# Half-size products for the first multiplication of two feed-forward steps of a one-core trunk

## The chip, the cores and the metric

One core of a Trainium2 chip runs the whole program in one launch. The metric is device time in microseconds, the median of several executions. "Before" is the kernel as it stands ahead of the change.

## The reference

The program is a two-layer trunk over 768 tokens (256 context tokens, then 512 latent tokens) with 1,024 channels. Each layer is a feed-forward half-step, a token mixer and a second feed-forward half-step. Layer 0 mixes by a diagonal state-space model (S5), layer 1 by gated linear attention (GLA). Around each of them stand an RMS norm and a modulation (scale, shift, gate) that comes from a product of a conditioning vector with `ada_w`. There are therefore four feed-forward steps. What matters here is

```python
def swiglu_ffn(h, w_in, w_out):
    gu = jnp.einsum('bld,df->blf', h, w_in)
    g, u = jnp.split(gu, 2, axis=-1)
    return jnp.einsum('blf,fd->bld', jax.nn.silu(g) * u, w_out)

def ffn_half_step(x, w_norm, shift, scale, gate, w_in, w_out):
    h = rmsnorm(x, w_norm) * (1.0 + scale) + shift
    return x + 0.5 * gate * swiglu_ffn(h, w_in, w_out)
```

with `w_in` 1,024 x 5,632 and `w_out` 2,816 x 1,024, all in 32-bit floats. Each operand of a large product is split into a rounded part and a remainder ("hi" and "lo"), and three matmuls (hi·hi, hi·lo, lo·hi) stand for one product.

## The kernel before

The activations lie transposed in SBUF: `xT` holds 8 tiles of 128 channels by 768 tokens. `Core.ffn` (L221) does one feed-forward step. It walks over 22 units of 128 hidden channels. `unit(j)` (L247) fetches the two weight tiles of a unit (gate and up, 128 x 1,024 each) by `weight` (L77): a DMA on the SP queue into one of four buffers `wraw`, a cast on ScalarE (L88) to a slot `whi`, and a subtraction on VectorE (L89) to a slot `wlo`. There are five slots of each kind, and three more while `core.more` is set, which it is from the S5 mixer's last product to the end of step three. `hidden(j, ...)` (L251) makes the gate and the up product of a unit for a stretch of tokens in two of the six PSUM banks, 8 x 3 matmuls each (`mm3`, L109 to L115), and then runs SiLU (L263), the product (L264), the cast (L265) and the remainder (L266). `products` (L268) multiplies the hidden channels of a group of units by `w_out` and adds the result to `xT` (L279). The units are taken in groups of four, twice in groups of two or four where the list `bounds` (L235) says so.

The first units, `lead` of them (4 with `core.more`), are made for thirds of the tokens (256 columns), so that they can begin on the first third while the norm of the others still runs. All later units work on halves (384 columns). The last group's second product is done third by third, and after each third the norm of the next step is queued.

That norm (`norm`, L186) squares the 8 tiles on ScalarE (L150) and adds the squares on VectorE (L151), forms the sums by a matmul with ones (L163), finds the inverse root in twelve small VectorE instructions (L167 to L175), spreads it over the partitions by a matmul (L182), scales (VectorE, L201), adds the shift and rounds (ScalarE, L218) and keeps the remainder (VectorE, L219). `later` and `tick` (L118 to L131) set where in the program these parts stand: so many ticks behind the third's last product. `ensure` forces them out before a unit reads their tokens.

Between the units a list of fillers runs (`fill`). In steps two and three they are the conditioning products, a block of 1,024 x 512 of `ada_w` each, done by `by_vector` (L416): four DMAs into `wraw` and 32 VectorE operations on it. Elsewhere the same blocks are done on TensorE (`block`, L410) by `ten(n)` (L1501). The S5 mixer ends in a recurrence on VectorE (`scan`, L824) and in `outputs` (L860), and then a gated product (`glu`, L921), whose last three of eight column groups are done third by third.

The framework orders the instructions of each engine ahead of time with a model of the timeline. The order in the program sets priorities, and the queues run in order on the chip.

## Time and profile before

| | us |
|---|---|
| median of 3 runs | 2894.43 |
| lowest, highest | 2892.82, 2896.95 |
| the profiled execution's own time | 2893.03 |
| its span | 2891.3 |

The profile is one execution. The time of an engine is "busy" only while an instruction runs on its data path. Matmuls overlap one another, so their rate is read from the distance of their starts and not from their duration. A line's idle time is the time its engine stood still just before it, put down to what came last. The work ahead of 998 us is step one, the S5 mixer and its gated product. Step two runs from 998 to 1554 us and step three from there to about 2125 us. GLA and step four follow.

### The profile page before, as it was taken

The page shows a single profiled execution, that of the slowest core. Times are in us where ns is not written, and L with a number is a line of the kernel's source. Part 1 is how long each engine was busy: PE and PEld are TensorE (multiplying, and loading weights), DVE is VectorE, ACT ScalarE, POOL GpSimd, SP SyncE. Part 2 cuts the span into 40 slices and gives each one's busy share as a digit, 9 for nine tenths or more (in the row PEclk, how much of TensorE's full clock was granted, in tenths as well). Part 3 has the DMA queues.
Part 4 walks back from the last instruction along what each step waited for, and adds up shares of the span by engine and source line. Part 5 has one row for each costly group of instructions (what it writes and reads, how often), then busy time and mean ns, then how long its engine had stood idle before and what let it go on. Part 6 is the DMA issues. An engine that isn't in the chain of part 4 may idle for free. (4 is left out here: it accounts for less than half of the span.)

```text
span 2891.3 us, 44942 instructions
## 1 busy us (share of the span) xinstructions
PE 2732.8 (95%) x18231; PEld 2581.4 (89%) x18231; DVE 1795.4 (62%) x4080; ACT 857.4 (30%) x1386; POOL 22.3 (1%) x57
## 2 busy tenths in 40 slices
PE   6999999996569999999999999999999999799998
PEld 5899999995459999999999999999988798788887
DVE  6699999536894565557527565665268786643433
ACT  4222222224363421111224221121246453332223
POOL 0000000000020000000000000000000000000000
PEclk9999999997789999999999999999999899799999
DMA  6545555526653133334211333333103112233330
GB/s 225 160 118 148 154 152 147 171 66 199 219 156 93 59 98 100 95 110 124 88 59 45 110 110 102 102 103 96 52 23 88 45 48 70 66 116 91 94 94 30
DMA packets 396044, 305.43 MB, mean 106 GB/s; under 512 B 57994, under 2 KB 344188, under 8 KB 395836
## 3 DMA queue, kind: packets, MB, share of 16 engines
q1 hardware_dynamic: 391228, 293.12, 34.7%
q10 hardware_dynamic: 4608, 9.44, 0.8%
q8 instruction: 143, 2.34, 0.3%
q14 instruction: 65, 0.53, 0.1%
HBM read 275.77 MB, written 30.41 MB: 106 GB/s over the span
## 5 line engine op out<-in xcount | busy, mean ns | idle before, releaser
L113 PE MATMUL bank<-h,whi 128*128 128x384 f32 (+3 forms) x3160 | 1044.7, 334 | 8.7 <-ACT whi L88 6.1
L114 PE MATMUL bank<-h,whi 128*128 128x384 f32 (+3 forms) x3160 | 1048.9, 333 | 0.0
L115 PE MATMUL bank<-h,wlo 128*128 128x384 f32 (+3 forms) x3160 | 1047.6, 332 | 0.0
L113 PEld LDWEIGHTS bank<-h,whi 128*128 128x128 f32 (+1 forms) x3160 | 593.9, 189 | 30.7 <-ACT whi L88 6.7
L88 ACT CAST whi<-wraw 128x1024 fp32r<-128x1024 f32 x313 | 327.4, 1048 | 966.3 <-PE bank L114 905.1
L114 PEld LDWEIGHTS bank<-h,whi 128*128 128x128 f32 (+1 forms) x3160 | 596.3, 189 | 17.2 <-issue 0.4
L115 PEld LDWEIGHTS bank<-h,wlo 128*128 128x128 f32 (+1 forms) x3160 | 595.1, 188 | 17.7 <-issue 0.7
L89 DVE TENSOR_TENSOR wlo<-wraw,whi 128x1024 fp32r<-128x1024 f32 x313 | 380.8, 1219 | 254.7 <-ACT whi L88 250.9
L114 PE MATMUL bank<-ml,whi 128*128 128x384 f32 (+2 forms) x1360 | 448.0, 330 | 0.0
L113 PE MATMUL bank<-mh,whi 128*128 128x384 f32 (+2 forms) x1360 | 445.7, 331 | 1.8 <-DVE xT L279 1.8
L115 PE MATMUL bank<-mh,wlo 128*128 128x384 f32 (+2 forms) x1360 | 446.2, 329 | 0.0
L279 DVE SCALAR_TENSOR_TENSOR xT<-bank,hg,xT 128x256 f32<-128x256 f32 (+2 forms) x488 | 221.4, 499 | 199.3 <-PE bank L115 198.8
L264 DVE TENSOR_TENSOR sg<-sg,bank 128x384 f32<-128x384 f32 (+2 forms) x166 | 89.4, 539 | 354.6 <-PE bank L115 339.2
L113 PEld LDWEIGHTS bank<-mh,whi 128*128 128x128 f32 x1360 | 256.3, 189 | 9.6 <-issue 2.8
L114 PEld LDWEIGHTS bank<-ml,whi 128*128 128x128 f32 x1360 | 256.9, 189 | 6.5 <-issue 0.4
L115 PEld LDWEIGHTS bank<-mh,wlo 128*128 128x128 f32 x1360 | 256.8, 189 | 6.2 <-issue 0.2
L427 DVE SCALAR_TENSOR_TENSOR adaacc<-wraw,cs,adaacc 128x512 f32<-128x512 f32 x336 | 236.9, 744 | 19.0 <-DMA wraw<-in_ada_w_dram 18.5
L265 ACT CAST mh<-sg 128x384 fp32r<-128x384 f32 (+2 forms) x166 | 83.5, 503 | 322.0 <-DVE sg L264 318.1
L263 ACT ACTIVATE sg<-bank 128x384 f32<-128x384 f32 (+2 forms) x166 | 79.5, 479 | 197.3 <-PE bank L115 195.1
L266 DVE TENSOR_TENSOR ml<-sg,mh 128x384 fp32r<-128x384 f32 (+2 forms) x166 | 89.8, 541 | 28.1 <-ACT mh L265 28.1
L150 ACT ACTIVATE sq<-xT 128x256 f32<-128x256 f32 (+1 forms) x126 | 52.0, 427 | 59.2 <-DVE xT L279 39.5
L201 DVE SCALAR_TENSOR_TENSOR nt<-xT,sc,bank 128x256 f32<-128x256 f32 (+2 forms) x136 | 61.8, 476 | 12.6 <-PE bank L182 9.7
(298 smaller groups left out, 2337.6 us busy)
## 6 DMA issues: line engine op xcount, KB each, us to landing
wraw<-in_ffn_w_in_dram SPq DMA_DIRECT2D x176, 512.0 KB, 4.2
wraw<-in_ada_w_dram SPq DMA_DIRECT2D x111, 512.0 KB, 4.0
wraw<-in_ffn_w_out_dram SPq DMA_DIRECT2D x88, 512.0 KB, 3.5
wraw<-in_gla_w_in_dram SPq DMA_DIRECT2D x24, 512.0 KB, 3.9
s5R<-s5r ACTq DMA_DIRECT2D x16, 512.0 KB, 4.9
s5O<-s5g SPq DMA_DIRECT2D x64, 128.0 KB, 3.8
wraw<-in_s_w_glu_dram SPq DMA_DIRECT2D x16, 512.0 KB, 6.5
big<-in_ada_w_dram SPq DMA_DIRECT2D x12, 512.0 KB, 8.8
```

What stands on the lines that cost most here:

```text
L88: nc.scalar.copy(out=hi[:, :n], in_=raw[:, :n])
L89: nc.vector.tensor_tensor(out=lo[:, :n], in0=raw[:, :n], in1=hi[:, :n].bitcast(F32), op=ALU.subtract)
L113: mm(out, wh, a[0], start=first, stop=False)
L114: mm(out, wh, a[1], start=False, stop=False)
L115: mm(out, wl, a[0], start=False, stop=last)
L201: nc.vector.scalar_tensor_tensor(out=t[:, a - s:z - s], in0=self.xT[:, k, a:z], scalar=sc[i][:, k:k + 1], in1=r[:, a - s:z - s], op0=ALU.m ...
L263: nc.scalar.activation(sg, banks[0][:, :e - s], AF.Silu)
L264: nc.vector.tensor_mul(sg, sg, banks[1][:, :e - s])
L265: nc.scalar.copy(out=mh[:, o], in_=sg)
L266: nc.vector.tensor_tensor(out=ml[:, o], in0=sg, in1=mh[:, o].bitcast(F32), op=ALU.subtract)
L279: nc.vector.scalar_tensor_tensor(out=self.xT[:, d, a:z], in0=banks[d][:, a - s:z - s], scalar=gate[i][:, d:d + 1], in1=self.xT[:, d, a:z], ...
L427: nc.vector.scalar_tensor_tensor(out=acc[:, v], in0=w[:, k], scalar=col, in1=acc[:, v], op0=ALU.mult, op1=ALU.add)
```

## The change

Steps two and three compute the first product by Strassen's scheme in Winograd's form: the weights of a unit are seen as a 2 x 2 block matrix (gate or up, by channels 0 to 511 or 512 to 1,023), the activations as a 2 x 2 block matrix (channel halves by even or odd blocks of 128 tokens). Seven half-size products (4 x 3 matmuls each) take the place of eight. A unit is done for all 768 tokens at once, 384 columns per matmul in three runs of 128, with each of the seven results in a bank of its own. GpSimd forms four sums of weight halves per unit, and in the norms ahead of the two steps it adds the squares and forms four differences of activations per half of a third. The sums of activations get a new buffer `hx`, and for it `core.more` goes: five weight slots of each kind stay. `lead` is 1, and the first unit is made for tokens 0 to 511 and then for 512 to 767. Blocks of `ada_w` are cut into four fillers each; steps two and three have six blocks each where they had eight, and the four others go to TensorE beside the S5 recurrence. The gated product's last part has two column groups where it had three.

```diff
+    def half(self, raw):
+        nc = self.nc
+        if self.pending is None:
+            self.pending = w = self.slot(True), self.slot(False)
+            hi, lo = (t[:, :HALF] for t in w)
+        else:
+            hi, lo = (t[:, HALF:] for t in self.pending)
+            self.pending = None
+        nc.scalar.copy(out=hi, in_=raw)
+        nc.vector.tensor_tensor(out=lo, in0=raw, in1=hi.bitcast(F32), op=ALU.subtract)
+        return hi, lo
...
-            nc.vector.tensor_add(acc, acc, sq)
+            (adds or nc.vector).tensor_tensor(out=acc, in0=acc, in1=sq, op=ALU.add)
...
+    def norm_seven(self, s, e, sc, sh, steps=0, gap=3):
+        acc = self.squares(s, e, nc.gpsimd)
...
+            for g in range(2):
+                v, w = (self.raw().rearrange("p (a i t) -> p a i t", i=2, t=t) for t in (2 * P, P))
+                for i in range(2):
+                    for lower in range(2):
+                        k, t = 4 * lower + 2 * g + i, v[:, lower, i]
+                        nc.vector.scalar_tensor_tensor(out=t, in0=self.xT[:, k, s:e], scalar=sc[:, k:k + 1], in1=r,
+                                                       op0=ALU.mult, op1=ALU.mult)
+                        nc.scalar.activation(t, t, AF.Identity, bias=sh[:, k:k + 1])
...
+                for x, minuend, less, (hi, lo) in ((b11, None, None, place(0, 0)), (t1, b12, b11, place(0, 1)),
+                                                   (t2, b22, t1, beside(0)), (b21, None, None, place(1, 0)),
+                                                   (t3, b22, b12, beside(1)), (b22, None, None, place(1, 1)),
+                                                   (t4, b21, t2, beside(2))):
+                    if less is not None:
+                        nc.gpsimd.tensor_tensor(out=x, in0=minuend, in1=less, op=ALU.subtract)
+                    nc.scalar.copy(out=hi, in_=x)
+                    nc.vector.tensor_tensor(out=lo, in0=x, in1=hi.bitcast(F32), op=ALU.subtract)
...
-        lead = 4 if self.more else 2
-        bounds = [0, 4, 8, 12, 14, 18, FT] if self.more else [0, 2, 6, 10, 14, 18, FT]
+        lead = 1 if seven else 4 if self.more else 2
+        bounds = [0, 4, 8, 12, 14, 18, FT] if self.more or seven else [0, 2, 6, 10, 14, 18, FT]
...
+            def both(out, i0, i1, op):
+                nc.gpsimd.tensor_tensor(out=out, in0=i0, in1=i1, op=op)
+                return self.half(out)
+            return [self.half(a11), both(a21, a21, a22, ALU.add), both(a11, a21, a11, ALU.subtract), self.half(a12),
+                    both(a21, a22, a11, ALU.subtract), both(a12, a12, a11, ALU.subtract), self.half(a22)]
...
+            nc.scalar.copy(out=g1, in_=part(0, 0))
+            p5 = part(1, 1)
+            plus(g2, g1, part(2, 4))
+            plus(g1, g1, part(3, 2))
+            nc.scalar.activation(g1, g1, AF.Silu)
+            plus(u1, g2, part(4, 5))
+            plus(g2, g2, p5)
+            plus(u2, u1, p5)
+            plus(g2, g2, part(5, 3))
+            nc.scalar.activation(g2, g2, AF.Silu)
+            nc.vector.tensor_mul(u2, u2, g2)
+            mid(u2, 1)
+            plus(u1, u1, part(6, 6))
+            nc.vector.tensor_mul(u1, u1, g1)
+            mid(u1, 0)
...
-            if j < KT - 3:
+            if j < KT - 2:
...
-            for j in range(KT - 3, KT):
+            for j in range(KT - 2, KT):
...
             s5.scan(sp, NX5, N5)
+            ten(1)
             s5.lagged()
-            ten(1)
+            ten(2)
             work = s5.outputs(sp, 3, yp, last)
-            ten(2)
+            ten(4)
             work()
...
-        with pool("more") as more:
-            core.more, core.nmore = more, 3
-            s5.glu(yp, halves, thirds, norm(0, 2, 12))
+        with pool("hx") as hx:
+            core.sums(hx)
+            s5.glu(yp, halves, thirds, norm_seven(0, 2, 12))
...
+            pieces = [(0, 512), (512, 768)]
...
-                ffn(0, 1, both, thirds, halves, thirds, mp,
-                    lambda: rest(8, mp) + [lambda: (mods.scale(1, 0), mods.half_gate(1, 0))], norm(1, 0))
-                ffn(1, 0, both, thirds, halves, thirds, mp,
+                ffn(0, 1, both, pieces, halves, thirds, mp,
+                    lambda: rest(6, mp) + [lambda: (mods.scale(1, 0), mods.half_gate(1, 0))], norm_seven(1, 0),
+                    spared=4, seven=True)
+                ffn(1, 0, both, pieces, halves, thirds, mp,
...
-                    norm(1, 1))
-            core.more = None
+                    norm(1, 1), spared=4, seven=True)
```

In `hidden_seven`, `part(i, op)` makes product i of the seven from the weight half i in 12 matmuls, `plus` is an addition on VectorE and `mid` the cast on ScalarE and the remainder on VectorE. `by_vector` returns its four DMAs and their VectorE work as four fillers.

## Rows read from the trace of the kernel before

**Rows 1.** The page, part 1: busy time, share of the span, instructions

```profile
PE 2732.8 (95%) x18231; PEld 2581.4 (89%) x18231; DVE 1795.4 (62%) x4080; ACT 857.4 (30%) x1386; POOL 22.3 (1%) x57
```

**Rows 2.** Windows: start:end, length, busy time per engine, granted clock, DMA share, GB/s

```profile
144.60:506.10 361.50, 361.50 (x2378) 345.59 (x2377) 335.08 (x797) 86.53 (x135) 3.69 (x7) 1.00 0.51 144
998.50:1554.20 555.70, 555.70 (x3500) 553.51 (x3499) 311.04 (x555) 129.16 (x206) 0.00 (x0) 1.00 0.31 92
1565.00:2100.00 535.00, 535.00 (x3315) 532.82 (x3314) 290.56 (x495) 117.17 (x183) 0.00 (x0) 1.00 0.32 91
```

**Rows 3.** Timeline of PE in step two (start, length): nine, then twelve distances

```profile
1002.78 0.28 PE L113 MATMUL bank<-h,whi 128*128 128x256 f32 x1
...
1003.83 0.28 PE L113 MATMUL bank<-h,whi 128*128 128x256 f32 x1
...
1099.80 0.33 PE L113 MATMUL bank<-h,whi 128*128 128x384 f32 x1
...
1101.89 0.34 PE L113 MATMUL bank<-h,whi 128*128 128x384 f32 x1
```

**Rows 4.** Groups of instructions by line and shape: busy us, mean ns, idle before

```profile
L89 DVE TENSOR_TENSOR wlo<-wraw,whi 128x1024 fp32r<-128x1024 f32 x312 | 380.4, 1222 | 252.0 <-ACT whi L88 248.2
L427 DVE SCALAR_TENSOR_TENSOR adaacc<-wraw,cs,adaacc 128x512 f32<-128x512 f32 x336 | 236.9, 744 | 19.0 <-DMA wraw<-in_ada_w_dram 18.5
L279 DVE SCALAR_TENSOR_TENSOR xT<-bank,hg,xT 128x256 f32<-128x256 f32 x208 | 96.2, 477 | 68.2 <-PE bank L115 67.9
L279 DVE SCALAR_TENSOR_TENSOR xT<-bank,hg,xT 128x384 f32<-128x384 f32 x120 | 69.6, 612 | 84.8 <-PE bank L115 84.7
L264 DVE TENSOR_TENSOR sg<-sg,bank 128x384 f32<-128x384 f32 x116 | 63.6, 549 | 232.4 <-PE bank L115 227.1 <-ACT sg L263 5.0
L218 ACT ACTIVATE h<-nt,mod 128x256 fp32r<-128x256 f32 x96 | 46.5, 505 | 46.4 <-DVE nt L201 41.2 <-DMA wraw<-in_ada_w_dram 4.8
L279 DVE SCALAR_TENSOR_TENSOR xT<-bank,hg,xT 128x128 f32<-128x128 f32 x120 | 40.8, 340 | 0.0
L266 DVE TENSOR_TENSOR ml<-sg,mh 128x512 fp32r<-128x512 f32 x18 | 12.3, 685 | 1.4 <-ACT mh L265 1.4
```

**Rows 5.** Timeline of DVE in step two: five operations in a row

```profile
1120.18 3.40 DVE L427 SCALAR_TENSOR_TENSOR adaacc<-wraw,cs,adaacc 128x512 f32<-128x512 f32 x5 [1.64 <-DMA wraw<-in_ada_w_dram]
```

**Rows 6.** Timelines of POOL and of DVE: one memset, then copies in S5

```profile
191.40 0.53 POOL L661 MEMSET s5cb<- 128x512 f32 x1 [170.24 <-PE aux L705]
...
817.42 2.33 POOL L890 COPY xs<-big 64x380 f32<-64x380 f32 x2 [5.64 <-PE bank L911]
...
817.59 2.63 DVE L890 COPY xs<-big 64x124 f32<-64x124 f32 x4 [0.46 <-PE bank L911]
...
823.56 1.33 DVE L890 COPY xs<-big 64x124 f32<-64x124 f32 x4
...
825.49 2.10 POOL L890 COPY xs<-big 64x380 f32<-64x380 f32 x2 [2.74 <-PE bank L911]
```

**Rows 7.** From step two to step three: two windows, timeline of DVE

```profile
1554.20:1558.60 4.40, 2.06 (x15) 1.90 (x14) 4.34 (x14) 2.18 (x5) 0.00 (x0) 0.90 0.55 158
1558.60:1565.00 6.40, 6.40 (x32) 6.40 (x33) 6.22 (x32) 3.13 (x7) 0.00 (x0) 0.54 0.17 59
...
1557.56 0.47 DVE L201 SCALAR_TENSOR_TENSOR nt<-xT,sc,bank 128x256 f32<-128x256 f32 x1
...
1565.45 0.48 DVE L219 SCALAR_TENSOR_TENSOR h<-nt,mod,h 128x256 fp32r<-128x256 f32 x1
```

**Rows 8.** End of the S5 recurrence: windows, timelines of DVE and PE

```profile
760.00:780.00 20.00, 14.03 (x84) 6.31 (x82) 17.66 (x115) 2.72 (x6) 0.00 (x0) 0.82 0.99 370
790.00:810.00 20.00, 0.00 (x0) 0.00 (x0) 20.00 (x128) 10.10 (x16) 0.00 (x0) 0.50 0.00 0
...
772.62 0.17 DVE L446 TENSOR_TENSOR mod<-aux,cols 128x8 f32<-128x8 f32 x1 [2.34 <-PE aux L406]
...
810.68 1.17 PE L911 MATMUL bank<-xs,wraw 128*128 128x96 f32 x4 [32.36 <-POOL xs L890]
```

117 lines of the change are left out of this document (93 added, 24 removed).

## The prediction, made before the changed kernel was run

> **What bounds the kernel.** I read the page's busy times first: TensorE is busy for 95% of the span, VectorE for 62%, ScalarE for 30%, GpSimd for 1% [rows 1]. A mean over stages proves little, so I took windows next. In steps two and three TensorE is busy for the whole of both stretches at the full clock, with VectorE at 311.0 of 555.7 us and at 290.6 of 535.0 [rows 2]. To see whether a busy TensorE is also working at its rate, I counted step two's matmuls and multiplied by the distance of their starts: nine distances take 1.05 us at 256 columns, 0.117 each, and twelve take 2.09 us at 384 columns, 0.174 each [rows 3]. A unit has 2 x 8 x 3 = 48 matmuls per stretch of tokens. Four lead units in thirds are 4 x 3 x 48 x 0.117 = 67.4 us, the 18 others in halves 18 x 2 x 48 x 0.174 = 301.0. The second product has 24 matmuls per unit and stretch: 18 units in halves, 150.5, and four in thirds, 33.7. Together 552.6 us against a window of 555.7 [rows 2]. So the two steps are matmul streams with nothing missing, and a matmul less is 0.174 us less, as long as the other engines keep up.
>
> **Part 1, fewer matmuls.** A unit takes 7 x 4 x 3 = 84 matmuls of 384 columns for 96: 14.6 us for 16.7. Twenty-one units are 307.3 us. The first unit is done in pieces, 84 x 0.117 = 9.8 for tokens 0 to 511, and for the last 256 tokens 84 matmuls of 128 columns. No row has that width with these types; the line through 256 and 384 columns [rows 3] gives 0.060 each, 5.0 us, and twice that bounds it above. First products per step: 368.4 before, 322.1 after, **-46.3, for two steps -92.6 us**.
>
> **Part 2, VectorE in a unit.** It must be covered by those 14.6 us. I reckon by groups of four units with their second product: 58.5 + 192 x 0.174 = 92 us on TensorE, 100 before. Operations in a row overlap: five of 744 ns take 3.40 us, 0.66 apart [rows 5], so I take 0.08 off each. Seven remainders of half-tiles (a 512-column subtraction takes 685 ns, one of 1,024 takes 1222 [rows 4]) replace two whole ones, and eleven operations of 384 columns (549 ns) replace four. Per group: 28 x 0.605 = 16.9, `w_out` 4 x 1.14 = 4.6, 44 x 0.47 = 20.7, updates of `xT` 8 x (0.40 + 0.26 + 0.53) = 9.5 [rows 4]. A conditioning block is 16 operations and four of like size, 20 x 0.66 = 13.3; six blocks over 22 filler calls, five calls per group, are 18. Sum 70 of 92 us, 76%. Before it was near 56% [rows 2]. Step one shows that this can be covered: there VectorE is busy for 335.1 of 361.5 us, 93%, and TensorE for all of it [rows 2]. I charge nothing; the cover is gone if VectorE needs more than 92 us.
>
> **Part 3, GpSimd in a unit.** Four two-input operations on 512 columns. The trace has none: a memset of that size takes 0.53 us, two copies of 380 columns 2.33 [rows 6], 1.57 each when scaled to 512, and 3.1 if a second input doubles it. I take 1.6, the nearest row in kind: 16 x 1.6 = 26 us per group, far under 92. What matters is what it does to VectorE. Four VectorE copies take 2.63 us while GpSimd copies and 1.33 us while it stands still [rows 6]: 1.3 lost in 2.33, or 56%. At that rate VectorE loses 0.56 x 26 = 14 us per group, 84 of 92, 91%, still inside what step one showed. Charge: nothing, up to the rival below. The Trainium skill ("SBUF — State Buffer", Who interferes with whom) states that a VectorE instruction with two SBUF inputs and a GpSimd instruction that reads SBUF exclude each other, the later one waiting for all of the earlier; by that rule the whole 26 us would come on top, 96 of 92 us, and each group would lose 4 us.
>
> **Part 4, the seams.** Before, the first unit needs one third of the norm. Now its first piece needs two, and a third's norm is longer: on ScalarE 8 shifts and 14 casts (505 ns [rows 4], 0.42 overlapped) for 8, on VectorE 22 operations for 16, and 8 differences on GpSimd in a chain, since each difference feeds the next. I take 10 us per third; 16 operations took from 1557.6 to 1565.9 [rows 7]. From step two to three the last product ends at 1554.2. The first third's norm then runs from 1557.5 to 1567.5, the second's to 1577.5, the third's, beside the first unit's own work, to 1590; the unit ends at about 1592, where 1554.2 + 14.8 = 1569 would be ideal: 23 us. Before, the seam cost 2.3 us of idle TensorE and 6.4 us at 0.54 of the clock, which is the lower of the two levels and loses 2.9: 5.2 [rows 7]. So **+18**. Between the gated product and step two TensorE stood still for nothing before [rows 2]; the same chain starts some 3 us sooner there: **+20**. Both together range from +8 (the order hides all but a third) to +60 (the GpSimd chain paces it). What is late next is the second unit's weights, since the norm takes the same `wraw` buffers; that is in the 1592. The seam to GLA keeps its norm.
>
> **Part 5, moved blocks.** Four of them go to TensorE beside the S5 recurrence. There TensorE stands still for 32.4 us until 810.7 [rows 8], and the DMA engines move nothing from 790 to 810. Their 16 transfers, 8.4 MB, pass on the SP queue the loads of `outputs` for later tiles, at 370 GB/s [rows 8] in 23 us. The cover is that idle stretch; the path is VectorE's recurrence, in whose queue each block puts one small addition, which waited 2.34 us for TensorE once [rows 8]. Four of them: 0.6 to 10 us; one wait in three, as in this stretch, gives **+4**. Taking them off VectorE in the steps saves nothing, as VectorE is not what ends there. The gated product's two column groups for three, and fillers in quarters, change 0.3 us: nothing.
>
> **Sum.** Against the profiled execution's 2893.0: -92.6 + 18 + 20 + 4 = -50.6, 2842.4. The median of the runs is 1.4 above that execution, so **2844 us**. A measurement of this kernel can tell about 0.2%, 6 us, from no change.
>
> **The rivals.**
> - *The seams are covered* (12%): the order made ahead of time brings the first two thirds forward, and about 8 us are left of 38: 2814. For it: before, the gated product's seam cost nothing. Against: two thirds must now be complete.
> - *The recurrence is held up* (10%): a block's addition waits for late DMAs, and all four in a row push the scan by some 22 us more: 2866. For it the wait of 2.34 us, against it the empty queue after 790 [rows 8].
> - *VectorE is late at times* (12%): it is 91% full and works in order; a unit then waits about one 512-column operation, 0.7 us x 42 = 30: 2874. Against: step one.
> - *GpSimd and VectorE exclude each other and VectorE becomes the bound* (8%): **slower**. Place: the weight sums in each unit, whose time is wholly VectorE's loss. It decides from (100 - 38/11 - 70)/16 = 1.7 us per GpSimd operation on, where a group has lost the whole gain. At 2.3 us a group takes 70 + 37 = 107 us, 15 over the forecast's 92, and eleven groups give +165: 3009. At 1.8 it is 2920. For it: the copies' 56% and the unknown price. Against: of VectorE's 70 us some 23 read a PSUM bank, and GpSimd need not come when VectorE is full. The page's rule named above is this case carried through.
> - *Fewer matmuls, same time* (3%): the right-hand sides are read in three runs of 128 columns, and if that makes 84 matmuls as long as 96, nothing is gained: 2936. The line through [rows 3] leaves no fixed cost per matmul, which speaks against it.
>
> **How the numbers follow.** The forecast has 55%. Its own range is 2822 to 2862. The range of 2808 to 2888 takes in the covered seams, the held recurrence and most of the late VectorE, and leaves out about 13%. Faster by over 0.2%: forecast, covered seams, recurrence and two thirds of the late VectorE, 85%. Slower: the two last rivals, 11%. Between: 4%.
>
> **What would show it.** Right: in the middle of steps two and three TensorE is busy throughout at full clock, matmuls of 384 columns start 0.174 us apart, and each step's stretch is some 46 us shorter but for the seams. At both seams the window after the last product shows TensorE idle for 10 to 20 us, with ScalarE and VectorE at the norm. VectorE stays under 92%. TensorE's wait before the S5 outputs shrinks, and their start moves by under 10 us. Wrong: VectorE full with TensorE waiting for it inside the units, GpSimd operations above 1.7 us, or 384-column matmuls further apart.

## The result, and the profile of the changed kernel

The changed kernel takes 2901.9 us, median of 20 runs, where the kernel before takes 2894.4 in 20 runs beside them: a ratio of 1.0025, 95% interval 1.0019 to 1.0031. It is slower by 7 us. The forecast was 2844 us, with a range that ended at 2888. The profiled execution of the changed kernel took 2896.56 us with a span of 2894.8, where the one before took 2893.03 and 2891.3. So the trace read below is 5 us shorter than the median of its kernel, and the one before 1.4.

The page of the changed kernel, part 1:

```profile
PE 2684.9 (93%) x17503; PEld 2513.8 (87%) x17503; DVE 2079.2 (72%) x4527; ACT 987.9 (34%) x1731; POOL 368.7 (13%) x323
```

Against [rows 1] TensorE has 728 matmul instructions less and is busy for 47.9 us less, yet the span grew. So it stands still, or works slowly, somewhere it did not before. To find where, look at the starts of TensorE's work behind an idle stretch (timeline of PE of the changed kernel; in brackets the idle time and what ended it; 1523.86 has none, it is the first matmul of step two's last group of second products):

```profile
811.94 1.17 PE L1049 MATMUL bank<-xs,wlo 128*128 128x96 f32 x4 [27.51 <-POOL xs L1028]
...
995.95 1.01 PE L178 MATMUL aux<-ones,ssq 128*128 128x1 f32 x4 [4.79 <-POOL ssq L166]
1003.00 1.22 PE L197 MATMUL bank<-ident,rs 128*128 128x128 f32 x4 [6.04 <-DVE rs L190]
1006.90 0.58 PE L128 MATMUL bank<-h,whi 128*128 128x256 f32 x1 [2.68 <-ACT h L274]
...
1038.46 0.69 PE L128 MATMUL bank<-h,whi 128*128 128x384 f32 x1 [5.02 <-DVE ssq L354]
...
1098.53 0.79 PE L128 MATMUL bank<-mh,whi 128*128 128x384 f32 x3 [2.96 <-ACT mh L350]
...
1523.86 0.28 PE L128 MATMUL bank<-mh,whi 128*128 128x256 f32 x1
...
1562.17 0.60 PE L178 MATMUL aux<-ones,ssq 128*128 128x1 f32 x4 [2.26 <-POOL ssq L166]
1571.19 1.22 PE L197 MATMUL bank<-ident,rs 128*128 128x128 f32 x4 [8.42 <-DVE rs L190]
1575.77 0.58 PE L128 MATMUL bank<-h,whi 128*128 128x256 f32 x1 [3.35 <-ACT h L274]
...
2128.87 0.35 PE L178 MATMUL aux<-ones,ssq 128*128 128x1 f32 x2 [2.34 <-DVE ssq L166]
```

The same places in the kernel before, where the last products of steps two and three end:

```profile
1557.79 0.56 PE L163 MATMUL aux<-ones,ssq 128*128 128x1 f32 x2 [2.34 <-DVE ssq L151]
...
2125.96 0.47 PE L163 MATMUL aux<-ones,ssq 128*128 128x1 f32 x3 [2.48 <-DVE ssq L151]
```

A start less its idle time is the end of the work before it, and so the stages can be set side by side:

| stretch | before | after | change | forecast |
|---|---|---|---|---|
| start to the S5 outputs | 810.7 | 811.9 | +1.3 | +4 |
| to step two's last product | 744.8 | 748.0 | +3.2 | -26.3 |
| to step three's last product | 568.0 | 566.6 | -1.4 | -28.3 |
| GLA and step four | 767.8 | 768.3 | +0.5 | 0 |

In this execution the moved blocks cost less than was charged. All that is missing is in the two steps, 29 and 27 us. Windows of the changed kernel: the first seam, 490 us inside step two, and the second seam (columns as in [rows 2]).

```profile
989.30:1045.00 55.70, 33.08 (x212) 31.23 (x213) 54.01 (x127) 33.30 (x87) 29.72 (x32) 0.75 0.23 66
1045.00:1535.00 490.00, 476.98 (x2743) 471.74 (x2742) 393.33 (x650) 154.58 (x274) 130.69 (x85) 0.99 0.30 90
1559.90:1610.00 50.10, 28.52 (x190) 27.06 (x190) 49.63 (x116) 30.34 (x82) 27.67 (x31) 0.75 0.18 52
```

The kernel before in the long one of these windows:

```profile
1045.00:1535.00 490.00, 490.00 (x2940) 487.81 (x2939) 273.04 (x450) 104.55 (x152) 0.00 (x0) 1.00 0.35 101
```

VectorE is busy for 80% of the 490 us. At the seams TensorE stands still for 22 us each, and its granted clock is 0.75 on average.

The matmul counts of the two long windows can't be set side by side, for 284 of the 2940 before and 93 of the 2743 now have 256 columns. A stretch that holds the same work in every unit runs from the first 384-column product of a unit to the last group's second product, in the changed kernel's step two from 1038.46 to 1523.86. In it are 2628 matmuls of 384 columns, in the kernel before 2400, and some small ones of the conditioning. Read in the same way from the PE timelines, it takes

| inside a step | matmuls | step two | step three | us per matmul |
|---|---|---|---|---|
| before | 2400 | 423.5 | 423.9 | 0.1765 |
| after | 2628 | 485.4 | 483.3 | 0.184 to 0.185 |

At the pace before, the 2628 would take 463.9 us. So 21 and 19 of the 29 and 27 us are lost inside the units, and the other 8 of each step at its seam.

What happens inside is to be read from VectorE's groups. The changed kernel, 1045 to 1535 us:

```profile
L562 DVE SCALAR_TENSOR_TENSOR adaacc<-wraw,cs,adaacc 128x512 f32<-128x512 f32 x82 | 72.6, 910 | 14.7 <-DMA wraw<-in_ada_w_dram 14.7
L351 DVE TENSOR_TENSOR ml<-nt,mh 128x384 fp32r<-128x384 f32 x42 | 33.3, 808 | 0.7
L354 DVE TENSOR_TENSOR nt<-nt,bank 128x384 f32<-128x384 f32 x42 | 22.8, 544 | 1.0 <-PE bank L130 1.0
L370 DVE TENSOR_TENSOR nt<-nt,sg 128x384 f32<-128x384 f32 x21 | 15.8, 754 | 0.3
L367 DVE TENSOR_TENSOR nt<-nt,ssq 128x384 f32<-128x384 f32 x21 | 15.0, 714 | 0.6 <-ACT ssq L366 0.6
```

Operations of 384 columns that read a PSUM bank take 544 ns, as the 549 of [rows 4]. Those of the same size with both inputs in SBUF take 714 to 808. The conditioning's operation took 744 ns in [rows 4] and takes 910. GpSimd's weight sums themselves, over the whole run, take 1.56 us on average, as the forecast has it (1.6), though the shortest take 1.28:

```profile
L324 POOL TENSOR_TENSOR wraw<-wraw 128x512 f32<-128x512 f32 x176 | 274.2, 1560 | 728.6 <-DVE wlo L113 355.0 <-DMA wraw<-in_ffn_w_in_dram 218.1 <-issue 48.4
```

One wait in detail, the one of 2.96 us that ends at 1098.53. Timelines of POOL (first line) and of DVE of the changed kernel:

```profile
1093.09 3.96 POOL L324 TENSOR_TENSOR wraw<-wraw 128x512 f32<-128x512 f32 x2 [5.06 <-DVE wlo L113]
...
1094.15 1.78 DVE L562 SCALAR_TENSOR_TENSOR adaacc<-wraw,cs,adaacc 128x512 f32<-128x512 f32 x1
1095.85 1.61 DVE L370 TENSOR_TENSOR nt<-nt,sg 128x384 f32<-128x384 f32 x1
1097.39 0.55 DVE L367 TENSOR_TENSOR nt<-nt,ssq 128x384 f32<-128x384 f32 x1
1098.04 1.03 DVE L351 TENSOR_TENSOR ml<-nt,mh 128x384 fp32r<-128x384 f32 x2
```

GpSimd is at two sums from 1093.09 to 1097.05, 3.96 us where the shortest take 1.28 each. The two operations that VectorE starts from 1094.15 on, while they run, take 1.78 and 1.61 us. The next, of the same size as the second, starts when GpSimd has ended and takes 0.55. The cast that TensorE waits for (L350, ScalarE) needs the result of the second. Both engines are held up, in turns. "Busy" hides it: the wait for the other engine counts as busy time.

### The profile page after: what moved, and what is told of

Read it like the earlier page. It is cut to its first block, busy times and chain, and to the rows that moved or that the text cites. A ratio compares the mean times of both kernels' runs of the same rounds, so it can differ in the third digit from the quotient of the medians.

```text
span 2894.8 us, 44887 instructions
## 1 busy us (share of the span) xinstructions
PE 2684.9 (93%) x17503; PEld 2513.8 (87%) x17503; DVE 2079.2 (72%) x4527; ACT 987.9 (34%) x1731; POOL 368.7 (13%) x323
## 3 DMA queue, kind: packets, MB, share of 16 engines
q8 instruction: 138, 2.26, 0.3%
## 5 line engine op out<-in xcount | busy, mean ns | idle before, releaser
L128 PE MATMUL bank<-h,whi 128*128 128x384 f32 (+2 forms) x2344 | 789.7, 342 | 23.0 <-DVE ssq L354 10.6
L129 PE MATMUL bank<-h,whi 128*128 128x384 f32 (+2 forms) x2344 | 797.2, 341 | 3.4 <-DVE h L275 2.7
L130 PE MATMUL bank<-h,wlo 128*128 128x384 f32 (+2 forms) x2344 | 795.4, 340 | 0.0
L128 PEld LDWEIGHTS bank<-h,whi 128*128 128x128 f32 x2344 | 442.2, 190 | 45.4 <-DVE ssq L354 10.9
L129 PEld LDWEIGHTS bank<-h,whi 128*128 128x128 f32 x2344 | 443.6, 189 | 23.1 <-DVE h L275 4.1
L130 PEld LDWEIGHTS bank<-h,wlo 128*128 128x128 f32 x2344 | 443.3, 189 | 17.8 <-issue 0.7
L91 DVE TENSOR_TENSOR wlo<-wraw,whi 128x1024 fp32r<-128x1024 f32 x225 | 277.4, 1234 | 161.4 <-ACT whi L90 153.5
L324 POOL TENSOR_TENSOR wraw<-wraw 128x512 f32<-128x512 f32 x176 | 274.2, 1560 | 728.6 <-DVE wlo L113 355.0
L112 ACT CAST whi<-wraw 128x512 fp32r<-128x512 f32 x308 | 180.7, 618 | 431.6 <-PE bank L129 253.9
L113 DVE TENSOR_TENSOR wlo<-wraw,whi 128x512 fp32r<-128x512 f32 x308 | 220.2, 740 | 34.9 <-ACT whi L112 34.2
L128 PE MATMUL bank<-hx,whi 128*128 128x384 f32 (+2 forms) x552 | 184.4, 334 | 0.0
L129 PE MATMUL bank<-hx,whi 128*128 128x384 f32 (+2 forms) x552 | 184.0, 334 | 0.0
L130 PE MATMUL bank<-hx,wlo 128*128 128x384 f32 (+2 forms) x552 | 183.8, 333 | 0.0
```

What stands on the lines that cost most here:

```text
L91: nc.vector.tensor_tensor(out=lo[:, :n], in0=raw[:, :n], in1=hi[:, :n].bitcast(F32), op=ALU.subtract)
L112: nc.scalar.copy(out=hi, in_=raw)
L113: nc.vector.tensor_tensor(out=lo, in0=raw, in1=hi.bitcast(F32), op=ALU.subtract)
L128: mm(out, wh, a[0], start=first, stop=False)
L129: mm(out, wh, a[1], start=False, stop=False)
L130: mm(out, wl, a[0], start=False, stop=last)
```

## The experiments

"The changed kernel" is 1.0025 [1.0019, 1.0031]; all ratios are against the kernel before on the same chip, with 95% intervals. 0.001 is 2.9 us.

### Inside the units: GpSimd's sums

**No sums.** The product lines read plain halves.

```diff
             def both(out, i0, i1, op):
-                nc.gpsimd.tensor_tensor(out=out, in0=i0, in1=i1, op=op)
                 return self.half(out)
```

> The changed kernel without GpSimd's four weight sums in each unit; the seven products then use the plain weight halves, so the outputs of steps two and three are not the reference's. GpSimd has no work in the units. Theory B (GpSimd's additions lengthen VectorE's operations, and so all waits inside the units): the remainder of a half tile goes back from 740 to some 685 ns, the products of two SBUF inputs from 755 towards 550, the waits at the groups and the one after the first unit (5.0 and 5.6 us) go: 30 to 40 us less than the changed kernel. Theory A (the dependency of the second product on the group's last unit): the chain is shorter by a few lengthened operations only, about 1 us of 2 to 4 at each of ten groups, and the seams stay: 5 to 14 us less.

2856.65 us, 0.9869 [0.9854, 0.9883]: 45 us less than the changed kernel, more than theory B's 30 to 40, and far from A. The run without sums, window from 1045 to 1535 us:

```profile
1045.00:1535.00 490.00, 488.96 (x2900) 486.42 (x2900) 360.41 (x669) 159.30 (x288) 12.96 (x17) 1.00 0.30 90
```

Three of its DVE groups in that window:

```profile
L353 DVE TENSOR_TENSOR nt<-nt,bank 128x384 f32<-128x384 f32 x42 | 23.0, 549 | 1.0 <-PE bank L130 1.0
L350 DVE TENSOR_TENSOR ml<-nt,mh 128x384 fp32r<-128x384 f32 x42 | 22.4, 553 | 0.9 <-ACT mh L349 0.3
L369 DVE TENSOR_TENSOR nt<-nt,sg 128x384 f32<-128x384 f32 x21 | 11.7, 556 | 0.3
```

808 and 754 ns have become 553 and 556, the PSUM form stays, and TensorE waits 1 us in all. The stretch inside a step takes 467.6 and 467.9 us, so 33 of the 45 us are gained there. Most of the rest is ahead of the second unit of each step, where TensorE waits 1.1 and 0.6 us for 5.0 and 5.6.

**Sums that nobody reads.** Was it the sharing, or that the casts waited for a sum?

```diff
+                junk = mids_pool.tile([P, HALF], mybir.dt.bfloat16, tag="junk", name="junk", bufs=1)
-                nc.gpsimd.tensor_tensor(out=out, in0=i0, in1=i1, op=op)
+                nc.gpsimd.tensor_tensor(out=junk, in0=i0, in1=i1, op=op)
                 return self.half(out)
```

> As the run without GpSimd's weight sums (the seven products use the plain weight halves, so the outputs of steps two and three are not the reference's), but GpSimd makes the four additions per unit all the same and writes them, in a 16-bit format, to a tile that nobody reads. No cast and no remainder waits for GpSimd any more, while its reads stand beside VectorE's work as in the changed kernel. Theory B (sharing: what GpSimd reads and writes lengthens VectorE's operations with two SBUF inputs, 803 ns beside it and 554 without it for the remainder of the hidden channels): the time goes back to the changed kernel's, 0.995 to 1.005 of the kernel before. Theory C (the weights come late because their casts wait for a GpSimd operation of 1.56 us): it stays at the level of the run without sums, 0.985 to 0.989.

2896.97 us, 1.0009 [0.9999, 1.0019]. 40 of the 45 us are back though in the window below nothing waits for GpSimd, neither an engine nor the DMA queue: theory B, and C falls. The run with unused sums, the same window:

```profile
1045.00:1535.00 490.00, 479.74 (x2753) 473.91 (x2752) 403.27 (x647) 152.89 (x272) 129.77 (x88) 0.99 0.30 90
```

Its groups of DVE and POOL in that window:

```profile
L352 DVE TENSOR_TENSOR ml<-nt,mh 128x384 fp32r<-128x384 f32 x42 | 28.5, 700 | 0.7 <-ACT mh L351 0.3
L325 POOL TENSOR_TENSOR junk<-wraw 128x512 bf16<-128x512 f32 x83 | 126.5, 1524 | 351.7 <-DMA wraw<-in_ffn_w_in_dram 346.7
```

**Copies that nobody reads.** One input for GpSimd where it had two.

```diff
+                junk = mids_pool.tile([P, HALF], mybir.dt.bfloat16, tag="junk", name="junk", bufs=1)
-                nc.gpsimd.tensor_tensor(out=out, in0=i0, in1=i1, op=op)
+                nc.gpsimd.tensor_copy(out=junk, in_=i0)
```

> The changed kernel with plain weight halves in the seven products, so the outputs of steps two and three are not the reference's, and in place of GpSimd's four sums four copies of one half tile each, written in a 16-bit format to a tile that nobody reads. Theory B1 (any read of SBUF by GpSimd holds up a VectorE operation with two SBUF inputs for as long as it lasts): VectorE's operations beside a copy are lengthened as they are beside a sum, to at most 1.6 us, and the time lies between the run without sums (0.987) and the one with unused sums (1.001) as the copy's duration lies between 0 and 1.53 us. Theory B2 (only two streams of reads by GpSimd hold it up): no VectorE operation is lengthened, and the time is that of the run without sums, 0.985 to 0.989.

2864.73 us, 0.9900 [0.9886, 0.9915]. Groups of DVE and POOL of this run, same window:

```profile
L352 DVE TENSOR_TENSOR ml<-nt,mh 128x384 fp32r<-128x384 f32 x42 | 24.3, 600 | 0.8 <-ACT mh L351 0.3
L325 POOL CAST junk<-wraw 128x512 bf16<-128x512 f32 x83 | 62.1, 749 | 396.9 <-DMA wraw<-in_ffn_w_in_dram 392.9
```

B1 in kind: a read with one stream also holds VectorE up, 600 ns for 553. In size it falls short: the copy is half as long as a sum and costs 9 us of the sums' 40. A copy differs from a sum in two things, its length and its one input, and no run tells which of them makes it so cheap.

**Less other work for VectorE.** The sums stay, most of the conditioning goes. (A conditioning block has 16 of these VectorE operations; the 32 in the description of the kernel is wrong.)

```diff
-                    else:
+                    elif not short:
                         nc.vector.scalar_tensor_tensor(out=acc[:, v], in0=w[:, k], scalar=col, in1=acc[:, v],
...
-            return [f for _ in range(n) for f in vec(*blocks.pop(0), pool)]
+            return [f for _ in range(n) for f in mods.by_vector(*blocks.pop(0), pool, True)]
```

> The changed kernel with 14 of the 16 VectorE operations of each conditioning block left out in steps two and three (the DMAs stay; the conditioning of layer 1 is wrong, and so is the output). VectorE's share in the body of the two steps falls from 79 to 82% to some 65%, while GpSimd's sums stay. Theory F (VectorE is too full, its own work and the time it waits out GpSimd's operations together): the waits of TensorE at the groups and after the first unit go, as they did without the sums, 25 to 45 us less than the changed kernel, 2857 to 2877. Theory K (what counts is the single operation that is held up in the chain from a unit's last product to the second product, however empty VectorE is): half or more of these waits stay, under 18 us less, above 2884.

2869.22 us, 0.9910 [0.9894, 0.9927], 33 us less than the changed kernel: theory F. The window of this run:

```profile
1045.00:1535.00 490.00, 487.53 (x2846) 484.97 (x2845) 345.05 (x585) 159.13 (x286) 126.26 (x94) 0.99 0.31 92
```

TensorE's waits in it (in total, times, longest):

```profile
PE bank L128 <- ACT mh L350: 1.4, 1, 1.4
PE bank L128 <- DVE nt L354: 1.0, 1, 1.0
```

The stretch inside a step takes 470.4 and 467.6 us, nearly as without the sums. So inside the units VectorE can afford to be held up at 70%, and at 80% it could not. The time is still 12 us above that of the run without sums. At least part of this lies at the second seam, where the first unit's piece of 128 columns took 17.4 us at a granted clock of 0.58 (in the changed kernel 9.6 us at 1.00). With less conditioning and no sums nothing was run.

**The sums on VectorE.** Nothing is left out here.

```diff
-                nc.gpsimd.tensor_tensor(out=out, in0=i0, in1=i1, op=op)
+                nc.vector.tensor_tensor(out=out, in0=i0, in1=i1, op=op)
```

> The changed kernel with the four weight sums of a unit on VectorE. Per unit VectorE gets four operations of 512 columns, 4 x 0.61 = 2.4 us more in a row, and is freed of what GpSimd costs it: its busy time in the changed kernel is 93 us above the run without sums, 2.1 us per unit. Theory B (VectorE's fill decides): about the same time as the changed kernel, within 12 us of it, with VectorE as full as there and GpSimd idle in the units. Theory C (the latency of GpSimd's operation decides): the sums come after 0.7 instead of 1.56 us, 20 to 40 us less than the changed kernel.

2868.94 us, 0.9920 [0.9905, 0.9934]: 30 to 33 us less than the changed kernel and 0.8% less than the kernel before. No kernel that leaves nothing out is faster. The window of this run:

```profile
1045.00:1535.00 490.00, 485.99 (x2850) 482.80 (x2850) 403.27 (x739) 158.81 (x283) 10.29 (x14) 0.99 0.30 91
```

The time is what theory C expected, and yet the unused sums had refuted C. What fails is B's claim that the busy time alone decides: VectorE is busy for 403.27 us here and in the run with unused sums, and 26 to 28 us lie between them. One difference is known: four operations of 683 ns stand where the order made ahead of time put them, whereas being held up comes where the two engines happen to meet. That this is the cause was not tried.

The stretch inside a step, in us, for the runs on the sums:

| run | step two | step three |
|---|---|---|
| changed kernel | 485.4 | 483.3 |
| unused sums | 487.1 | 483.9 |
| sums on VectorE | 473.3 | 475.7 |
| less conditioning | 470.4 | 467.6 |
| unused copies | 470.0 | 469.3 |
| no sums | 467.6 | 467.9 |

So the sums cost 6 to 8 us per step on VectorE, at 82% and with nothing to hold it up, and 15 to 20 on GpSimd, at 80 and 82%.

### Inside the units: the second product's order

```diff
+                    if seven and d0 + dw <= 4:
+                        if d0 + dw == 4:
+                            products(ws, 0, 4, dw, f0, f1, *parts[0])
+                            for d in (0, 2):
+                                products(ws, d, d + 2, dw, f0, f1, *parts[1])
+                        continue
```

> The changed kernel, but in each group the second product begins with four output tiles for the first half of the tokens instead of two, so that 4 x 3 x 3 = 36 matmuls (6.3 us) instead of 18 (3.1 us) lie between the group's last unit and the first matmul that needs that unit's result. Theory A (structure): a unit that is done for all 768 tokens at once leaves nothing to work on while its own chain of additions, SiLU, cast and remainder ends, and TensorE waits for it at every group: in the changed kernel's trace these waits and the slower matmuls behind them are 16 us in step two and 14 us in step three. A says they vanish, 20 to 30 us less than the changed kernel, some 2870 to 2882. Theory B (VectorE is late because GpSimd's additions lengthen its operations): VectorE stays as late as before and TensorE meets the same wait one chunk or one unit further on: less than 8 us gained.

2906.89 us, 1.0044 [1.0029, 1.0059]: no gain, theory A fails. The trace says why. In the changed kernel TensorE ends the group's last first product at 1084.6 and fills the time to 1095.4 with 54 second-product matmuls of the first three units, not 18: the order made ahead of time had already stretched the chunk, and with the edit the number is 54 again, with a wait of 2.95 us for 2.96. So the last unit's result came 14 us behind its last product. That is lateness, not a short cover.

The same edit on the run with the sums on VectorE:

> The run with the weight sums on VectorE, and the second product begins with four output tiles for the first half of the tokens, as in the first run of all. With GpSimd out of the units, waits for a group's last unit are left in one group of each step, the one that holds two units, 3.6 us and the slower matmuls behind it, 5 to 8 us per step. Theory A (the last unit's chain has too little work to hide behind): doubling that work takes 4 to 12 us off the run with the sums on VectorE, 2857 to 2865. Theory B (what was wrong there was VectorE's lateness alone, and it is now gone but for the place where its work is densest): within 4 us of that run.

2870.68 us, 0.9921 [0.9906, 0.9936]. Nothing again, theory B; the group of two units still waits (2.55 us, 2.66 without the edit).

### The seams: how much work VectorE has

**Squares back on VectorE.**

```diff
-        acc = self.squares(s, e, nc.gpsimd)
+        acc = self.squares(s, e)
```

> The changed kernel with the additions of squares ahead of steps two and three back on VectorE. Theory A3 (the chain of seven GpSimd additions of 781 ns each holds up the seams): the waits for the sums of squares, 4.8 us ahead of step two and 2.3 ahead of step three, shrink to 2 us or less, and up to 6 us are gained in all. Theory A4 (VectorE is the full engine of the seams, busy for 12.9 of 13.0 us): 21 additions of 0.4 us more for it at each seam make both seams longer, 3 to 10 us lost.

2902.87 us, 1.0029 [1.0017, 1.0041], no change: neither. The wait for the sums ahead of step two is gone, the one ahead of step three stays (2.79 us for 2.26), and the stretches inside the steps, where nothing was edited, are 3 us longer each. So the run doesn't part the two theories.

**No differences.**

```diff
-                        nc.gpsimd.tensor_tensor(out=x, in0=minuend, in1=less, op=ALU.subtract)
+                        x = minuend
```

> The changed kernel without the norm's differences of activations: GpSimd's eight subtractions per third are left out and the casts read the plain halves, so the outputs of steps two and three are not the reference's. Theory S3 (the chain of GpSimd differences, 0.86 us each, is what makes the seams long): the waits behind the spread of the root shrink and each seam is 6 to 12 us shorter, 12 to 24 us less than the changed kernel in all. Theory S1 or S2 (the norm's own VectorE work and the two thirds): under 6 us in all.

2892.21 us, 0.9995 [0.9985, 1.0004], 9 us less than the changed kernel for both seams, between the two expectations. But something else moved against it: the first unit's piece of 128 columns took 15.9 and 16.8 us at the two seams, at a granted clock of 0.63 and 0.62, where the changed kernel has 10.8 and 9.6 at 1.00. These are 12 us. Without them the gain would be some 21 us, which is in S3's range; so S3 doesn't fall by this run.

**No GpSimd at all**, on the run with the sums on VectorE.

```diff
-        acc = self.squares(s, e, nc.gpsimd)
+        acc = self.squares(s, e)
...
-                        nc.gpsimd.tensor_tensor(out=x, in0=minuend, in1=less, op=ALU.subtract)
+                        nc.vector.tensor_tensor(out=x, in0=minuend, in1=less, op=ALU.subtract)
```

> The run with the weight sums on VectorE, and in the two norms the additions of squares and the differences of activations on VectorE as well, so that GpSimd has no work left in steps two and three. Theory B carried to the seams (a VectorE operation with two SBUF inputs waits out GpSimd's operation, also the root's operations on two columns, which take 0.68 instead of 0.15 us there): in the 13 us in which the first two thirds are scaled and split GpSimd works for most of the time, 16 operations of 0.83 us; on VectorE the same take 16 x 0.36 = 5.8 us, and its stalls go: 4 to 8 us gained at each seam, 2853 to 2861 us. Theory S2 (VectorE is full at the seams and any operation more there is lost time): 16 x 0.36 + 14 x 0.3 = 10 us more for it per seam, 5 to 10 us lost at each, 2879 to 2889.

2880.37 us, 0.9951 [0.9935, 0.9968], 9 to 11 us more than with the sums alone on VectorE, in theory S2's range. At the second seam of this run the second third's spread waits 11.18 us, 8.22 with GpSimd's help:

```profile
1564.78 1.22 PE L197 MATMUL bank<-ident,rs 128*128 128x128 f32 x4 [11.18 <-DVE rs L190]
```

At the first seam the clock has a part in the loss: the piece of 128 columns took 18.3 us at a granted clock of 0.67, 10.0 at 1.00 in the run it is compared with. As a whole GpSimd's help is worth its price at the seams, and in the units it is not; that more work for VectorE is the reason shows at the second seam alone, by that wait.

Then with the longer first chunk of the second product as well:

> Both together: no GpSimd work in the two steps, and the longer first chunk of the second product. If the effects are independent, the sum of the two runs' gains against the run with the weight sums on VectorE, within 4 us. If the order made ahead of time shifts the seams as it did where single edits moved the end of the gated product by 4 to 6 us, up to 6 us beside it.

2877.07 us, 0.9948 [0.9929, 0.9968]. The two edits' changes add up to 2868.9 + 11.4 + 1.7 = 2882; it is 5 us below that, between the two allowances (by the ratios it is 1 us below). Nothing in it asks for a third effect.

**No remainders of the activations**, on the run with the sums on VectorE; in `hidden_seven` both operands are part 0.

```diff
                     nc.scalar.copy(out=hi, in_=x)
-                    nc.vector.tensor_tensor(out=lo, in0=x, in1=hi.bitcast(F32), op=ALU.subtract)
```

> The run with the weight sums on VectorE, without the remainders of the activations in the norms ahead of steps two and three: 14 VectorE operations of 0.36 to 0.42 us per third are left out, and the products read the rounded part in the remainder's place, so the outputs of the two steps are not the reference's. Theory S2 (the seams are as long as VectorE's work in them): 3 x 14 x 0.36 = 15 us less VectorE work per seam, of which the two thirds ahead of the first product make 10; each seam is 8 to 14 us shorter, 2841 to 2853 us. Theory S4 (the seams are as long as the chain of the second third, its root, spread, scale and shift, whatever VectorE does beside it): the root's small operations still wait their turn, under 5 us per seam, 2859 to 2869.

2859.62 us, 0.9872 [0.9856, 0.9889], 9 to 14 us less: at the lower edge of S4. Two windows at the first seam of this run:

```profile
1000.00:1012.00 12.00, 3.67 (x14) 3.21 (x14) 11.02 (x34) 9.15 (x28) 8.01 (x13) 0.50 0.00 0
1012.00:1024.00 12.00, 11.83 (x79) 11.32 (x78) 5.88 (x15) 11.21 (x31) 8.50 (x13) 0.76 0.10 28
```

VectorE is free for half of the second one, and TensorE still stands still for most of the first: 15 us less work per seam bought 5 to 7. Work is a part of the seam; what the rest is, this run doesn't show.

### The seams: the order of the thirds

**Sum of squares half a third sooner**, ahead of step two only.

```diff
-            s5.glu(yp, halves, thirds, norm_seven(0, 2, 12))
+            s5.glu(yp, halves, thirds, norm_seven(0, 2, 6))
```

> The changed kernel, but ahead of step two each third's sum of squares is put 6 instead of 12 ticks behind the third's end, so half a third sooner, as the gated product's last part has 8 ticks per third where it had 12. Theory A1 (the seam is long because the norm of the first third is queued late): the first third's norm is done before the gated product ends, and the 29 us lost from 989 to 1038 fall by 5 to 8 us. Theory A2 (what counts is the second third, whose squares can only be formed after the gated product's last matmuls but one third, and the work of VectorE as a whole): less than 3 us either way.

2916.75 us, 1.0078 [1.0061, 1.0095], 15 us lost: neither. The gated product ended at 995.4 for 989.3, but the S5 outputs had begun 5.5 us later, ahead of the edit. Behind it TensorE's first product came 2 us sooner. Then it waited 3.16 us ahead of the piece of 128 columns and did it at a granted clock of 0.51, in 21.4 us for 10.8, so that the second unit began 8 us later behind the gated product than in the changed kernel.

**Only a piece's own thirds forced out**, with the sums on VectorE.

```diff
+    def only(self, token):
+
+        while any(item[2] < token for item in self.queue):
+            i = [item[2] < token for item in self.queue].index(True)
+            self.queue.pop(i)[1]()
...
-            self.ensure(e)
+            (self.only if seven else self.ensure)(e)
```

> The run with the weight sums on VectorE, and ahead of a piece only the norms of its own thirds are forced out, so that the last third's spread and split come behind the first piece's products (in TensorE's order 84 matmuls further back) and not ahead of them. Theory S4 (the last third's norm takes VectorE from the first two): TensorE begins up to 5 us sooner at each seam and the first piece runs through, 2859 to 2866. Theory S2 (all of VectorE's work is due by the end of the first unit, in whatever order): what is gained ahead of the first piece is lost ahead of the second, 2865 to 2880.

2896.0 us, 1.0002 [0.9992, 1.0012], 24 to 27 us lost, more than either theory held. Windows of this run:

```profile
1023.00:1031.00 8.00, 2.45 (x9) 1.72 (x7) 7.98 (x16) 7.46 (x22) 5.62 (x7) 0.64 0.01 2
1031.00:1041.00 10.00, 9.65 (x45) 9.65 (x46) 8.57 (x19) 3.25 (x8) 0.80 (x2) 0.50 0.71 211
```

TensorE stands still a second time, ahead of the last third, and works through the piece of 128 columns behind it at the lower clock: 22.2 and 22.3 us at the two seams, where the run it is compared with has 10.0 and 9.5. That is about all of the loss.

**Three pieces.**

```diff
-            pieces = [(0, 512), (512, 768)]
+            pieces = thirds
```

> The changed kernel with the first unit made in three pieces of 256 tokens, so that the first needs one third of the norm instead of two. Theory S1 (the seams are long because two thirds of the norm must be complete ahead of the first product): TensorE begins some 10 to 15 us sooner at each seam; against that two more pieces of 128 columns take the place of one of 256 and each costs what the last piece costs, 84 x 0.110 = 9.2 us where the wide one takes 9.8 in all, so 8.7 us more per step. 4 to 14 us gained over the two steps. Theory S2 (VectorE is full throughout the seam, so that the first product of all tokens comes at the same time however they are cut): nothing is gained, 5 to 17 us lost.

2945.72 us, 1.0181 [1.0164, 1.0198], 44 us lost, more than either theory held. TensorE did begin sooner, and its idle time from 930 to 2150 us fell from 72 us in the changed kernel to 42. But the small matmuls were twice as long as expected. Windows of this run:

```profile
1006.00:1016.00 10.00, 10.00 (x49) 10.00 (x48) 6.50 (x30) 2.44 (x5) 0.80 (x2) 0.50 0.00 0
...
1056.00:1066.00 10.00, 10.00 (x47) 10.00 (x47) 3.86 (x10) 2.91 (x6) 2.49 (x2) 0.50 0.35 100
```

Two matmul starts of its PE timeline:

```profile
1007.46 0.42 PE L128 MATMUL bank<-h,whi 128*128 128x128 f32 x1
1007.67 0.41 PE L129 MATMUL bank<-h,whi 128*128 128x128 f32 x1
```

They start 0.21 us apart at a granted clock of 0.50, for as long as they last, with TensorE busy.

**The small piece first**, with the sums on VectorE.

```diff
-            pieces = [(0, 512), (512, 768)]
+            pieces = [(0, 256), (256, 768)]
```

> The run with the weight sums on VectorE, with the first unit's pieces the other way about: tokens 0 to 255 first, then 256 to 767. The first piece needs one third of the norm, and as many matmuls of 128 and of 256 columns are made as before. Theory S1 (the seams are long because two thirds must be normed ahead of the first product): TensorE begins 7 us sooner ahead of step two and 13 sooner ahead of step three, works through the 84 small matmuls while the other thirds are normed, and each seam is 4 to 8 us shorter: 2853 to 2861. Theory L (in the run with three pieces the matmuls of 128 columns that came behind an idle TensorE stood 0.213 us apart at a granted clock of 0.50, and the clock did not rise for 60 us until the wide ones began): the first piece takes 84 x 0.213 = 18 us, the second begins at half clock too, and the seams are as long as they were or longer: 2865 to 2885.

2894.01 us, 1.0003 [0.9993, 1.0013], worse than theory L's 2885. Windows of this run:

```profile
1000.00:1010.00 10.00, 10.00 (x49) 10.00 (x48) 5.99 (x29) 2.26 (x4) 0.37 (x1) 0.50 0.00 0
1010.00:1020.00 10.00, 7.47 (x35) 7.18 (x34) 5.57 (x17) 3.65 (x11) 1.26 (x2) 0.50 0.00 0
```

Its PE timeline at the end of the first piece:

```profile
1027.36 0.89 PE L128 MATMUL bank<-h,whi 128*128 128x256 f32 x2 [9.88 <-DVE h L275]
```

The first piece ran at half clock, as L says. Beside it VectorE had time, 58% busy, but the other thirds' spreads stood in TensorE's queue behind all 84 matmuls, and TensorE then waited 9.88 us.

**Spreads where their data are ready**, with the sums on VectorE; then the same with the small piece first.

```diff
-            s5.glu(yp, halves, thirds, norm_seven(0, 2, 12))
+            s5.glu(yp, halves, thirds, norm_seven(0, 2, 3, 1))
...
-                    lambda: rest(6, mp) + [lambda: (mods.scale(1, 0), mods.half_gate(1, 0))], norm_seven(1, 0),
+                    lambda: rest(6, mp) + [lambda: (mods.scale(1, 0), mods.half_gate(1, 0))], norm_seven(1, 0, 3, 1),
```

> The run with the weight sums on VectorE, and ahead of both steps each third's sum of squares stands 3 ticks behind the third's end (12 and 9 before) and its spread one tick later (3 before). In TensorE's order the spread of the second third then comes ahead of the last third's last product, and no longer behind the last third's sum of squares. Theory S4 (the seams are as long as the order in the queues makes them): the second third is normed while the last third's products run, TensorE begins 8 to 14 us sooner at each seam, 2845 to 2858. Theory S2 (VectorE's work decides, in whatever order): the same work comes sooner but delays the last third's updates; under 4 us per seam, 2861 to 2877.

> The same, with the first unit's small piece first. In TensorE's order the last third's spread now comes after 24 of the first piece's 84 matmuls and not behind all of them, which was the 9.9 us of waiting in the run with the small piece first. Theory S4: that wait goes, and as the first piece follows the last product without a pause the clock need not fall: 2850 to 2865. Theory L (matmuls of 128 columns behind an idle TensorE stay at half clock): if TensorE is idle for some us ahead of the first piece, it takes 18 us again, and the time stays above 2868.

2889.2 us, 0.9982 [0.9973, 0.9991], and 2887.76 us, 0.9977 [0.9967, 0.9986]. In the first neither S4's range nor S2's is met. In the second S4 fails too and L holds: its small piece, behind idle times of 2.48 and 1.94 us, took 22 and 24 us at granted clocks of 0.52 and 0.54. The first of the two, TensorE's starts behind idle time:

```profile
978.16 1.20 PE L197 MATMUL bank<-ident,rs 128*128 128x128 f32 x4 [3.72 <-DVE rs L190]
...
999.13 1.22 PE L197 MATMUL bank<-ident,rs 128*128 128x128 f32 x4 [5.67 <-DVE rs L190]
...
1010.25 0.39 PE L128 MATMUL bank<-h,whi 128*128 128x256 f32 x1 [2.70 <-ACT whi L112]
1012.33 0.58 PE L130 MATMUL bank<-h,wlo 128*128 128x256 f32 x1 [1.58 <-DVE wlo L113]
```

The spread now holds up the gated product in TensorE's queue, and behind the norms the first unit's weights (`whi`, `wlo`) are late, which share ScalarE, VectorE and `wraw` with them. The waits have moved, and the piece of 128 columns ran at a granted clock of 0.61 at both seams, 18.7 and 16.6 us.

## Why the prediction was wrong

**Part 1 held.** Matmuls of 384 columns start 0.174 us apart as before. Without GpSimd's sums the stretch inside a step takes 0.178 us per matmul, which makes 94.0 us for a group of 528; before it was 0.1765 and 101.7 for 576. That is 7.6% less, of the 8.3% that fewer matmuls can give. One term was off: matmuls of 128 columns are 0.110 us apart behind a busy TensorE (the forecast took 0.060, with twice that as bound), 4.2 us per step.

**Part 2 held as a count and failed as a rule.** VectorE was put at 76% of a group without GpSimd; it was 360 of 490, 74%. The step that failed is "I charge nothing; the cover is gone if VectorE needs more than 92 us". VectorE never was full: 80% in the changed kernel, less than the 91% that the forecast allowed. TensorE waited all the same. Step one's 93% [rows 2] was no proof for these units: with the sums on VectorE, where nothing holds it up, 82% already goes with a loss of 6 to 8 us per step. Why step one can bear more is not shown.

**Part 3: a price that fits by luck, and a wrong consequence.** A sum takes 1.56 us (1.6 forecast), but in that mean is the time for which GpSimd itself is held up; the shortest take 1.28. The step "Charge: nothing, up to the rival below" lost 40 to 45 us, by the two runs without and with unused sums. The scale from the copies, 56% of GpSimd's time lost by VectorE, was too high if anything: VectorE's busy time grew by 2079.2 - 1985.9 = 93 us (the second number from the page of the run without sums) beside 274 us of sums, a third. The rival "GpSimd and VectorE exclude each other" had 8% and its place right, but it was made to begin at 1.7 us per operation, with VectorE full. It is there at 1.56 us and 80%, and at 70% inside the units it is all but gone. What makes 80% too much is argued and not shown: an operation that is held up stands, as at 1095.85 above, in the chain that TensorE waits for. In the rival's terms, "VectorE is late at times" (30 us, 12%) came nearest in size, against 33 us inside the units.

The rule that the prediction cited, the Trainium skill ("SBUF — State Buffer", Who interferes with whom), says that a VectorE operation with two SBUF inputs and a GpSimd operation that reads SBUF take turns, and that one with at most one SBUF input is not touched unless it runs in one of its faster modes. The traces agree on both: 553 ns on average without the sums and up to 1649 beside one for the remainder of the hidden channels, 544 to 549 whether beside or not where one input is a PSUM bank. Carried through as the prediction did, 4 us for each of eleven groups, it gives 44 us; the run without sums gives 45. The agreement is partly luck, for VectorE lost a third of GpSimd's time and not all of it, and only 33 of the 45 us are inside the units.

**Part 4: the sum came out, by errors that cancel, once the sums are gone.** In the changed kernel the first product after step two came 15.9 us behind the last one (1575.77 against 1559.91), where the forecast had 23. But the first unit ended at 1601.6, 41.7 us behind instead of 37.8: its first piece took 16.2 us for 9.8, at a granted clock of 0.72, and its last 9.6 for 5.0. The clock behind an idle TensorE is what was left out. TensorE then waited 5.6 us for VectorE. Its idle time, 22 us a seam, was just above the forecast's 10 to 20. In the run without sums the two steps take 723.0 and 545.0 us, 9.8 us more than the forecast's 718.5 and 539.7 in the terms of the first table. 7.7 of these are inside the units (467.6 and 467.9 for 463.9 at the pace before), so that Part 4's +38 came out 2 us too small. In the changed kernel 15 us are missing at the seams, and the run without sums gets 13 of them back.

**Part 5** was +1.3 for +4 in this execution. In the profiles of the 18 runs, whose edits all stand behind that place in the program, the S5 outputs begin between 809.8 and 819.4 us, 815.2 in the median, which is 4.5 behind the 810.7 before. So the charge was right, as far as single executions tell.

So of the 58 us between forecast and measured time, 45 are GpSimd's sums. Without them 2856.65 us stand against 2844. Of these 13 us 8 are inside the units, and the others are spread over the rest.

What stays open is why a matmul inside a unit costs 0.178 us for 0.1765 when the sums are gone, and how a seam's 22 us divide between VectorE's work and the order. Less work helped a little (9 us without the differences, 9 to 14 without the remainders, for both seams), more work hurt (9 to 11), and of six other orders none was faster. But these runs do not hold the clock still. In the changed kernel the first unit's 84 matmuls of 128 columns took 10.8 and 9.6 us at the two seams, at a granted clock of 1.00. In each of the six orders such a piece ran wholly or mostly at the lower level at every seam that the edit touched, in 17 to 24 us. So it did at both seams of the run without differences, and at the first seam of the two runs without GpSimd. With the waits inside the piece this is 5 to 14 us per seam, as much as any of the effects that were looked for.

## What to carry to other kernels

Before work goes to GpSimd, list what VectorE does beside it: operations with both inputs in SBUF can have to wait out GpSimd's (here 714 to 808 ns on average for 553), those that read PSUM did not (544 for 549). Do not clear such an offload by VectorE's mean busy share; in the units here the same four additions cost 30 to 33 us less on VectorE itself than on GpSimd, at a busy share that was no lower (82% for 80%). When a run tries another order, compare the granted clock behind the idle stretches too, before the order is judged by the time. When a trace shows one line's operation at two durations, look at the other engine's timeline at the longer ones.

## What the runs showed of the hardware that was not expected

- Even operations on two columns are held up: the root's small operations take 0.14 to 0.17 us alone, and 23 of the 37 in the two seams and steps that meet a GpSimd operation take 0.49 us or more, most of them 0.5 to 0.7. Among them is a scaling with one SBUF input only (L186, 0.70 us at 993.16). The one that reads PSUM (L182) is not held up, 0.15 or 0.16 us beside GpSimd. Nor are the transposes of the conditioning: 704 ns with the sums and 706 without.
- In the run with three pieces 128-column matmuls kept TensorE busy for 56 of the 60 us from 1006 to 1066, at a granted clock of 0.50, the lower of the two levels, throughout; 84 of them are 18 us at that pace. In the changed kernel the same ones behind 256-column matmuls ran at a granted clock of 1.00, 0.110 us apart, which makes 9.2. Splitting a unit finer to start sooner can cost the clock.
- At full clock 128 columns are hardly cheaper than 256: 0.110 us for 0.117.
